# The gate and up products of a transformer layer by Strassen's seven block products in place of eight

## The chip, the cores and the metric

The kernel runs on one core of a Trainium2 chip. Its time is the device time of one launch in microseconds (us), the median of several runs. The engines are named as the profile names them: PE is TensorE's matmuls, PEld its weight loads, DVE is VectorE, ACT is ScalarE, POOL is GpSimd, and SP issues the DMAs.

## What is computed

The reference is a block of two trunk layers over 512 latent tokens and 256 context tokens of width 1024. Each layer has a mixing part (four head groups and an output projection) and a feed-forward part; the change lies in the feed-forward of the last layer, which handles the latent tokens alone:

```python
def swiglu(h, wg, wu, wd):
    return (jax.nn.silu(h @ wg) * (h @ wu)) @ wd

x = x + g2 * swiglu(modulate(rms_norm(x, g_ffn[l]), sh2, sc2), w_gate[l], w_up[l], w_down[l])
```

Here h is 512 x 1024, w_gate and w_up are 1024 x 2816 and w_down is 2816 x 1024, all in float32.

## The kernel before, in words

Activations lie feature-major: 128 features on the partitions, tokens along the free dimension. A float32 product is made of three matmuls (`mm3`, lines 63 to 67): each operand is split into a high part in the rounded format that TensorE takes (a copy on ScalarE) and a low part (the difference, on VectorE), and high x high, high x low and low x high are added up in PSUM. Weights are loaded into `raw` (three buffers of 128x512) and split into `w` tiles (six buffers, each with the high and the low part of 128x512); `wsplit`, lines 75 to 85, does both. Line 82 is the high part on ACT, line 83 the low part on DVE (in parts of the mixing on POOL). `split_to` (lines 91 to 93) does the same for data already in SBUF.

In the output projection of the mixing part (lines 917 to 924) eight column tiles `mt` are made one after the other. For each of them `residual` (line 911) adds the product to the stream, `Squares` (lines 284 and 285) adds up the squares for the norm, and `scaled` (lines 255 to 258) puts out the token tile `st` of 128 features, scaled, in high and low parts, with two columns that carry the shift. The norm's factor r is multiplied in behind the products, since it depends on the token alone.

The feed-forward (lines 941 to 977) goes in three blocks of hidden column tiles, 8, 7 and 7 of the 22 (`BLOCKS`, line 24). For each column tile `ft` it splits the gate and the up weights (four `w` tiles), and for the last layer each of the two products runs over eight feature tiles and two token halves of 256 and 258 columns, three matmuls each: 96 matmuls for a column tile. Lines 949 to 958 take the products out of PSUM, multiply by r, apply SiLU, add the shifts, multiply gate by up, and split the result into a hidden tile `h`. After a block follow the down products (lines 966 to 971), eight column tiles of 512 columns over the block's hidden tiles.

The order of the instructions on each engine is written by a scheduler ahead of time from the program's order, the buffers and its own estimates; on the chip each engine then runs its list in order and waits by semaphores. PSUM's eight banks are handed out in turn (`psum_any`).

Of the kernel before, what the change touches and what calls it, by code (L numbers as in the profile page):

```python
# [17 lines left out]
KT = 8  # L18
# [21 lines left out]
def hybrid_block(ctx: ExitStack, tc, t, out):  # L40
# [221 lines left out]
    def scaled_proj(w, h, cuts, pss, k):
        for (c0, c1, *_), ps in zip(cuts[0], pss):
            mm3(ps[:, :c1 - c0], wf(w, k, 0), wf(w, k, 1), h[:, 0, c0:c1], h[:, 1, c0:c1], k == 0, k == KT - 1)

    def shift_of(cuts, pss):
        sh = small.tile([128, 2], F32, tag="sh", name="sh")
# [119 lines left out]
    for l in range(DEPTH):  # L387
# [529 lines left out]
        for mt in range(KT):  # L917
            w = wsplit(t["wout"][l, mt])
            outs = proj_out(w, KT, mh, ORDER, [[["pj", "pj", "tq", "md", "sc", "sc", "pt", "po"], ["pj", "pj", "tq", "md", "sc", "sc", "pt", "po"]][l][(mt * len(segs) + i) % 8] for i in range(len(segs))])
            x = xs[mt]  # L920
            residual(x, outs, per_feature(m, 2, mt))
            sq.add(x)
            sh = per_feature(m, 3, mt)
            h.append(scaled(x, a[:, 1, mt], sh[:, 0:1].to_broadcast([128, 2]) if last else sh, segs))

        turn[0] = 0
        r = norm_spread(norm_scale(sq, segs), segs, ("po", "pt"))
# [12 lines left out]
        work = steps()  # L940
        for b0, b1 in BLOCKS:
            hid = []
            for ft in range(b0, b1):
                gu = [wsplit(t["wg"][l, ft]), wsplit(t["wu"][l, ft])]
                gps, ups = [[psum_any() for _ in range(2)] for _ in range(2)]
                for w, pss in zip(gu, (gps, ups)):
                    for k in range(KT):
                        scaled_proj(w, h[k], cuts, pss, k)
                shg, shu = shift_of(cuts, gps), shift_of(cuts, ups)
                hd = tile("h", [128, 2, NT], F32R)  # L950
                for (_, _, s0, s1, v, o), g_, u_ in zip(cuts[0], gps, ups):
                    n = s1 - s0
                    sg, up = tile("post", [128, 512])[:, :n], tile("post", [128, 512])[:, :n]
                    V.tensor_mul(sg, g_[:, o:o + n], r[:, s0:s1])
                    S.activation(sg, sg, AF.Silu, bias=shg[:, v:v + 1])
                    V.tensor_mul(up, u_[:, o:o + n], r[:, s0:s1])
                    V.scalar_tensor_tensor(up, up, shu[:, v:v + 1], sg, op0=OP.add, op1=OP.mult)
                    split_to(hd[:, 0, s0:s1], hd[:, 1, s0:s1], up)
                for _ in range(3):
                    next(work, None)  # L960
                hid.append(hd)
            final = b1 == FFT
            if final:
                sq = Squares(segs)
                hu = []
            for mt in range(KT):
                n = b1 - b0
                w = wsplit(t["wd"][l, mt][:, b0:b1].rearrange("p k c -> p (k c)"))
                outs = proj_out(w, n, hid, range(n))
                x = xs[mt]  # L970
                residual(x, outs, per_feature(m, 5, mt))
                if final and last:
                    nc.sync.dma_start(out[:, mt], x[:, :SEQ])
                elif final:
                    sq.add(x)
                    nc.sync.dma_start(xdram[:, mt], x[:, :SEQ])
                    hu.append(scaled(x, mods[1]["a"][:, 0, mt], mods[1]["m"][:, mt // 4, 0, mt % 4], segs))
# [45 lines left out]
def _layouts(i):  # L1023
# [42 lines left out]
    o["win_dv"] = featmajor(i["w_in"][:, :, 1792:2048], KT).reshape(L, 2, 128, 1024)  # L1066
    wo = np.concatenate([i["w_out"][:, swap], i["w_out"][:, 256:]], 1)
    o["wout"] = featmajor(wo, KT).reshape(L, KT, 128, 1024)
    o["wg"] = featmajor(i["w_gate"], KT).reshape(L, FFT, 128, 1024)
    o["wu"] = featmajor(i["w_up"], KT).reshape(L, FFT, 128, 1024)  # L1070
    o["wd"] = featmajor(i["w_down"], FFT)
    for n in ("a_q_gain", "a_k_gain", "d_q_gain", "d_k_gain", "a_sink", "b_v_gain"):
        o[n] = ac(i[n])
# [27 lines left out]
```

## Time and profile before

| | |
|---|---|
| median of 3 runs | 1574.88 us (1571.65 to 1575.27) |
| profiled execution | 1574.71 us, its span 1572.9 us |
| TensorE's mean granted clock | 0.987 of full speed |
| busy share of PE, DVE, ACT, POOL | 97%, 60%, 40%, 7% |
| matmuls | 10,210 |
| DMA | 163.42 MB, mean 104 GB/s |

An engine's busy share is a mean over the whole span; what bounds a stage is read from the stage. The profile's time of a matmul is longer than the distance to the next, since they are pipelined: the distance between starts is what a matmul costs. The same holds for operations of VectorE and ScalarE in a dense stretch.

### The profile page before, as it was taken

How to read it: one execution, taken by the hardware profiler on the slowest of the kernel's cores; microseconds unless marked ns; L12 is line 12 of the kernel's file. 1: busy time of each engine (PE TensorE's matmuls, PEld its weight loads, DVE VectorE, ACT ScalarE, POOL GpSimd, SP SyncE). 2: the span in 40 equal slices, each digit the busy share in tenths (PEclk: the TensorE clock that was granted, in tenths of full speed). 3: DMA queues.
4: the chain of work that ended last, by engine and by line, in shares of the span. 5: the costliest groups of instructions: out<-in, count | busy, mean ns of one | idle time of the engine just before them, and what ended most of it. 6: DMA issues, size and time to landing. Idle time of an engine off the chain costs nothing.

```text
span 1572.9 us, 26447 instructions
## 1 busy us (share of the span) xinstructions
PE 1531.0 (97%) x10210; PEld 1348.2 (86%) x10210; DVE 950.5 (60%) x2325; ACT 628.3 (40%) x1305; POOL 116.2 (7%) x107
## 2 busy tenths in 40 slices
PE   7889999999999999999999998799999999999999
PEld 4678888788888888888888887798879998998997
DVE  4796867586485624833384467878856543454453
ACT  5545665543322112221222344457654332332331
POOL 2430200000000000000000005622000000000000
PEclk9899999999999999999999999999999999999999
DMA  8342133442243323622272231212223233223223
GB/s 308 121 128 85 50 126 107 134 138 81 83 145 111 117 61 114 223 57 69 90 245 64 79 118 41 71 42 73 69 61 102 94 88 101 95 83 106 94 82 101
DMA packets 79326, 163.42 MB, mean 104 GB/s; under 512 B 12000, under 2 KB 17760, under 8 KB 79200
## 3 DMA queue, kind: packets, MB, share of 16 engines
q1 hardware_dynamic: 79200, 161.73, 32.4%
q8 instruction: 80, 1.31, 0.3%
q14 instruction: 46, 0.38, 0.1%
HBM read 157.50 MB, written 4.19 MB: 103 GB/s over the span
## 4 chain that ended last, share of the span: by engine, by line
PE 88%; DVE 7%; DMA 3%; ACT 1%; issue 1%; SPq 0%; ACTq 0%; DVEq 0%
PE pj L65 9%; PE pj L67 9%; PE pj L66 9%; PE sc L66 6%; PE sc L65 6%; PE sc L67 6%; PE tq L65 3%; PE tq L66 3%; PE tq L67 3%; PE po L66 3%; PE po L65 3%; PE po L67 3%; PE po L351 3%; PE pt L66 2%; PE pt L67 2%; PE pt L65 2%
## 5 line engine op out<-in xcount | busy, mean ns | idle before, releaser
L82 ACT ACTIVATE w<-raw 128x512 fp32r<-128x512 f32 x368 | 227.4, 622 | 632.6 <-PE sc L67 157.3
L83 DVE TENSOR_TENSOR w<-raw,w 128x512 fp32r<-128x512 f32 x336 | 227.9, 681 | 244.8 <-ACT w L82 244.4
L65 PE MATMUL pj<-w,h 128*128 128x256 f32 x480 | 142.5, 297 | 14.7 <-DVE post L498 8.4
L66 PE MATMUL pj<-w,h 128*128 128x256 f32 x480 | 141.1, 294 | 1.5 <-DVE w L83 1.5
L67 PE MATMUL pj<-w,h 128*128 128x256 f32 x480 | 141.3, 295 | 0.0
L65 PE MATMUL pj<-st,w 128*128 128x258 f32 (+2 forms) x384 | 120.5, 314 | 0.9 <-ACT st L255 0.7
L66 PE MATMUL pj<-st,w 128*128 128x258 f32 (+2 forms) x384 | 120.2, 313 | 1.1 <-DVE st L256 1.1
L65 PE MATMUL sc<-st,w 128*128 128x258 f32 (+2 forms) x384 | 119.9, 312 | 0.0
L66 PE MATMUL sc<-st,w 128*128 128x258 f32 (+2 forms) x384 | 119.9, 312 | 0.0
L67 PE MATMUL pj<-st,w 128*128 128x258 f32 (+2 forms) x384 | 119.5, 312 | 0.0
L67 PE MATMUL sc<-st,w 128*128 128x258 f32 (+2 forms) x384 | 118.9, 310 | 0.0
L65 PEld LDWEIGHTS pj<-w,h 128*128 128x128 f32 x480 | 95.9, 200 | 18.7 <-DVE post L498 9.2
L66 PEld LDWEIGHTS pj<-w,h 128*128 128x128 f32 x480 | 95.9, 200 | 3.3 <-DVE w L83 1.7
L67 PEld LDWEIGHTS pj<-w,h 128*128 128x128 f32 x480 | 95.4, 199 | 3.1 <-issue 3.0
L83 POOL TENSOR_TENSOR w<-raw,w 128x512 fp32r<-128x512 f32 x32 | 42.3, 1338 | 722.7 <-ACT w L82 715.4
L65 PEld LDWEIGHTS pj<-st,w 128*128 128x128 f32 x384 | 73.0, 190 | 8.0 <-ACT st L255 1.9
L66 PEld LDWEIGHTS pj<-st,w 128*128 128x128 f32 x384 | 72.9, 190 | 5.9 <-DVE st L256 1.3
L67 PEld LDWEIGHTS pj<-st,w 128*128 128x128 f32 x384 | 72.7, 190 | 5.6 <-issue 1.7
L65 PEld LDWEIGHTS sc<-st,w 128*128 128x128 f32 x384 | 73.1, 190 | 4.7
L66 PEld LDWEIGHTS sc<-st,w 128*128 128x128 f32 x384 | 72.9, 190 | 4.1
L67 PEld LDWEIGHTS sc<-st,w 128*128 128x128 f32 x384 | 72.4, 189 | 4.1
L65 PE MATMUL po<-st,w 128*128 128x512 f32 (+1 forms) x192 | 66.6, 347 | 0.0
(310 smaller groups left out, 4153.4 us busy)
## 6 DMA issues: line engine op xcount, KB each, us to landing
mraw<-in_wmod SPq DMA_DIRECT2D x80, 512.0 KB, 3.6
raw<-in_wg SPq DMA_DIRECT2D x88, 256.0 KB, 2.6
raw<-in_wu SPq DMA_DIRECT2D x88, 256.0 KB, 2.6
raw<-in_wd SPq DMA_DIRECT2D x64, 256.0 KB, 2.7
h<-in_wslab SPq DMA_DIRECT2D x16, 512.0 KB, 7.9
raw<-in_wout SPq DMA_DIRECT2D x32, 256.0 KB, 2.7
x<-in_xt SPq DMA_DIRECT2D x16, 384.0 KB, 5.5
raw<-in_wd SPq DMA_DIRECT2D x32, 192.0 KB, 2.4
```

What stands on the lines that cost most here:

```text
L65: T.matmul(ps, ah, bh, start=start, stop=False)
L66: T.matmul(ps, ah, bl, start=False, stop=False)
L67: T.matmul(ps, al, bh, start=False, stop=stop)
L82: S.activation(w[:, 0, :n], raw, AF.Copy)
L83: eng.tensor_sub(w[:, 1, :n], raw, w[:, 0, :n].bitcast(F32))
L351: T.matmul(o[64 * hh:64 * hh + 64, :128], vs[hh][lo:hi], pts[i, hh], start=i == 0, stop=i == n - 1)
```

## The change

For the last layer each pair of column tiles is handled at once. The weights of a pair form a 2x2 block matrix (two halves of the features by two column tiles), the tokens another one (two halves of the features by two halves of the tokens). The products of the blocks are made by Strassen's scheme in Winograd's form, seven products of sums and differences of blocks in place of eight products of blocks. To this end:

- The host's layout of the gate and up weights puts the feature tiles of one half next to each other, so that a 128x512 piece is one block. Layer 0 reads the same layout with another index (`at`).
- `token_blocks` and `token_forms` take the place of `scaled`: the four token blocks go into an `mraw` tile, GpSimd makes four differences of them (128x258) in a second one, and the seven operands are split into high and low parts.
- `weight_forms` loads the four weight blocks of a pair (two into an `mraw` tile in one DMA of 512 KB, two into `raw` tiles), makes four sums and differences of 128x512 on GpSimd in `pts` tiles (three buffers), and splits seven operands.
- `strassen` runs seven products of four feature tiles, three matmuls of 258 columns each, and puts four results together with seven additions out of PSUM on VectorE and one copy on ScalarE.
- The blocks of column tiles become 8, 8 and 6, for both layers.

Shortened:

```diff
-BLOCKS = ((0, 8), (8, 15), (15, 22))
+BLOCKS = ((0, 8), (8, 16), (16, 22))
...
+    def token_blocks(par, x, gain, sh, b):
+        S.activation(by128(b[:, 2 * par:2 * par + 2, 0:HN]), halves(x), AF.Copy, scale=gain[:, 0:1])
+        for h in (2 * par, 2 * par + 1):
+            V.tensor_copy(b[:, h, HN:HN + 2], sh[:, 0:1].to_broadcast([128, 2]))
+
+    def token_forms(b, single):
+        u = tile("mraw", [128, 4, HN + 2])
+        G.tensor_sub(u[:, 1], b[:, 1], b[:, 0])
+        G.tensor_sub(u[:, 2], b[:, 3], u[:, 1])
+        G.tensor_sub(u[:, 0], b[:, 2], u[:, 2])
+        G.tensor_sub(u[:, 3], b[:, 3], b[:, 1])
+        f1 = tile(single, [128, 1, 2, HN + 2], F32R)
+        f2 = tile("st", [128, 3, 2, HN + 2], F32R)
+        f3 = tile("st", [128, 3, 2, HN + 2], F32R)
+        for f, i, src in ((f2, 0, b[:, 2:4]), (f1, 0, b[:, 0:1]), (f3, 0, u[:, 1:4]), (f2, 2, u[:, 0:1])):
+            n = src.shape[1]
+            split_to(f[:, i:i + n, 0], f[:, i:i + n, 1], src)
...
+    def weight_forms(src):
+        both = load_raw(src[0], "mraw")
+        a11, a12 = both[:, 0:512], both[:, 512:1024]
+        a21, a22 = [load_raw(src[1][:, c:c + 512], "raw", 512) for c in (0, 512)]
...
+        yield parts(a12)
+        yield parts(a11)
+        s1 = comb(G.tensor_add, a21, a22)
+        yield parts(s1)
+        s2 = comb(G.tensor_sub, s1, a11)
+        yield parts(s2)
+        yield parts(comb(G.tensor_sub, a12, s2))
+        yield parts(a22)
+        yield parts(comb(G.tensor_sub, a11, a21))
+
+    def strassen(src, forms):
+        wfs = weight_forms(src)
+        n = HN + 2
+        def product(p):
+            ps = psum_any()[:, :n]
+            w = next(wfs)
+            for kk, f in enumerate(forms):
+                mm3(ps, w[:, 0, 128 * kk:128 * kk + 128], w[:, 1, 128 * kk:128 * kk + 128], *f[p],
+                    kk == 0, kk == len(forms) - 1)
+            return ps
+        c1, c2 = tile("post", [128, 2, n]), tile("post", [128, 2, n])
+        u = tile("br", [128, n])
+        p2, p1 = product(2), product(1)
+        S.activation(u, p1, AF.Copy)
+        V.tensor_add(c1[:, 0], p2, u)
+        p5, p6 = product(5), product(6)
+        V.tensor_add(u, p6, u)
+        V.tensor_add(c1[:, 1], p5, u)
+        p3 = product(3)
+        V.tensor_add(c1[:, 1], p3, c1[:, 1])
+        p4, p7 = product(4), product(7)
+        V.tensor_add(c2[:, 0], p7, u)
+        V.tensor_add(c2[:, 1], p5, c2[:, 0])
+        V.tensor_add(c2[:, 0], p4, c2[:, 0])
+        return c1, c2
...
-            h.append(scaled(x, a[:, 1, mt], sh[:, 0:1].to_broadcast([128, 2]) if last else sh, segs))
+            if not last:
+                h.append(scaled(x, a[:, 1, mt], sh, segs))
+                continue
+            if mt % 2 == 0:
+                blocks = tile("mraw", [128, 4, HN + 2])
+            token_blocks(mt % 2, x, a[:, 1, mt], sh, blocks)
+            if mt % 2:
+                h.append(token_forms(blocks, "T" if mt < 6 else "bias"))
...
+            for ft in range(b0, b1, 2) if last else ():
+                rv = halves(r)
+                gate = strassen([t["wg"][l, ft], t["wg"][l, ft + 1]], h)
+                for c in gate:
+                    cv = c[:, :, 0:HN]
+                    V.tensor_mul(by128(cv), by128(cv), rv)
+                    S.activation(cv, cv, AF.Silu, bias=c[:, 0, HN:HN + 1])
+                up = strassen([t["wu"][l, ft], t["wu"][l, ft + 1]], h)
+                for c, g_ in zip(up, gate):
+                    cv = c[:, :, 0:HN]
+                    V.tensor_mul(by128(cv), by128(cv), rv)
+                    V.scalar_tensor_tensor(cv, cv, c[:, 0, HN:HN + 1], g_[:, :, 0:HN], op0=OP.add, op1=OP.mult)
+                    hd = tile("h", [128, 2, NT], F32R)
+                    split_to(halves(hd[:, 0]), halves(hd[:, 1]), by128(cv))
+                    hid.append(hd)
```

In the lists that follow a row is one instruction with the line of the kernel that issues it, what it writes and reads by tile names, its shape, and the engines or DMA queues that it waits for; x2 stands for two alike.

VectorE in the middle of a gate/up stretch, one column tile of before (`w` are low halves of weights, line 954 and 956 the products with the norm, 957 gate by up):

```order
L83 TENSOR_TENSOR w<-raw,w 128x512 [waits DMAHW4_49,Activation_49]
L954 TENSOR_TENSOR post<-pj,row 128x256 [waits PE_49]
L268 COPY sh<-pj 128x2 [waits PE_49]
L83 TENSOR_TENSOR w<-raw,w 128x512 [waits DMAHW5_49,Activation_49]
L83 TENSOR_TENSOR w<-raw,w 128x512 [waits DMAHW6_49,Activation_49]
L956 TENSOR_TENSOR post<-sc,row 128x256 [waits PE_49]
L954 TENSOR_TENSOR post<-pj,row 128x256 [waits DVE_49]
L268 COPY sh<-sc 128x2 [waits PE_49]
L956 TENSOR_TENSOR post<-sc,row 128x256 [waits DVE_49]
L957 SCALAR_TENSOR_TENSOR post<-post,sh 128x256 [waits DVE_49]
L83 TENSOR_TENSOR w<-raw,w 128x512 [waits DMAHW7_49,Activation_49]
L957 SCALAR_TENSOR_TENSOR post<-post,sh 128x256 [waits DVE_49,Activation_49]
```

and the same place now, the second half of a pair (348 to 357 are the additions out of PSUM, 1054 the product with the norm, 1055 gate by up, `w<-pts` the low half of a sum that GpSimd made):

```order
L93 TENSOR_TENSOR w<-pts,w 128x512 [waits Activation_49]
L353 TENSOR_TENSOR post<-sc,post 128x258 [waits DVE_49,PE_49]
L1054 TENSOR_TENSOR post<-post,row 128x2x256 [waits DVE_49]
L93 TENSOR_TENSOR w<-pts,w 128x512 [waits Activation_49]
L1055 SCALAR_TENSOR_TENSOR post<-post 128x2x256 [waits DVE_49]
L93 TENSOR_TENSOR w<-pts,w 128x512 [waits Activation_49]
L355 TENSOR_TENSOR post<-pt,br 128x258 [waits PE_49]
L93 TENSOR_TENSOR w<-raw,w 128x512 [waits DMAHW6_49,Activation_49]
L356 TENSOR_TENSOR post<-pj,post 128x258 [waits DVE_49]
L93 TENSOR_TENSOR h<-post,h 128x2x2x128 [waits Activation_49]
L357 TENSOR_TENSOR post<-tq,post 128x258 [waits DVE_49]
L93 TENSOR_TENSOR w<-pts,w 128x512 [waits Activation_49]
```

Of twelve rows before, four are low halves of weights. Of twelve now five are, four of them of what GpSimd wrote, and four are additions of 128x258 with one input in PSUM.

GpSimd before, from its last work in the last layer's mixing part (low halves of projection weights, bias tiles) to the end of the program:

```order
L625 TENSOR_TENSOR bias<-dmask,br 128x256 [waits DMAHW1_49,DVE_49]
L625 TENSOR_TENSOR bias<-dmask,br 128x192 x2
L83 TENSOR_TENSOR w<-raw,w 128x512 [waits DMAHW0_49,Activation_49]
L83 TENSOR_TENSOR w<-raw,w 128x512 [waits DMAHW2_49,Activation_49]
L83 TENSOR_TENSOR w<-raw,w 128x512 [waits DMAHW3_49,Activation_49]
L1096 UNCONDITIONAL_BRANCH
L1096 ISA [waits barrier_Pool_Activation_PE_DVE_SP_gather]
```

and now, from the differences of the last token blocks into the first weight sums (`mraw<-mraw` token blocks, `pts` weight sums):

```order
L292 TENSOR_TENSOR mraw<-mraw 128x258 [waits DVE_49,Activation_49,Pool_49]
L293 TENSOR_TENSOR mraw<-mraw 128x258 [waits Activation_49,Pool_49]
L295 TENSOR_TENSOR mraw<-mraw 128x258
L294 TENSOR_TENSOR mraw<-mraw 128x258 [waits Pool_49]
L318 TENSOR_TENSOR pts<-pts,mraw 128x512 [waits DMAHW1_49,PE_49]
L318 TENSOR_TENSOR pts<-mraw,pts 128x512 [waits PE_49,Pool_49]
L318 TENSOR_TENSOR pts<-mraw,raw 128x512 [waits DVE_49]
L318 TENSOR_TENSOR pts<-raw 128x512 [waits DMAHW0_49,DMAHW3_49,DVE_49,Pool_49]
L318 TENSOR_TENSOR pts<-pts,mraw 128x512 [waits DMAHW2_49,DVE_49,Pool_49]
L318 TENSOR_TENSOR pts<-mraw,pts 128x512 [waits DVE_49,Pool_49]
```

Before, GpSimd's list ends with the projections of the mixing part; now eighty-eight weight sums follow, eight for each pair of column tiles.

SP's loads where the output projection passes into gate/up, before:

```order
L72 DMA raw<-in_wout 128x512 [waits DMAHW4_49,DMAHW0_49,DVE_49]
L72 DMA raw<-in_wout 128x512 [waits DMAHW5_49,DMAHW2_49,DVE_49]
L72 DMA raw<-in_wg 128x512 [waits DMAHW6_49,DMAHW3_49,DVE_49]
L72 DMA raw<-in_wg 128x512 [waits DMAHW7_49,DMAHW4_49,DVE_49]
L72 DMA raw<-in_wu 128x512 [waits DMAHW5_49,DVE_49]
L72 DMA raw<-in_wu 128x512 [waits DMAHW6_49,DMAHW1_49,DVE_49]
L72 DMA raw<-in_wg 128x512 [waits DMAHW7_49,DVE_49]
L72 DMA raw<-in_wg 128x512 [waits DMAHW0_49,DVE_49]
```

and now:

```order
L72 DMA raw<-in_wout 128x512 [waits DMAHW4_49,DMAHW0_49,DVE_49]
L72 DMA raw<-in_wout 128x512 [waits DMAHW5_49,DMAHW2_49,DVE_49]
L72 DMA raw<-in_wg 128x512 [waits DMAHW6_49,DMAHW3_49,DVE_49]
L72 DMA raw<-in_wg 128x512 [waits DMAHW7_49,DMAHW4_49,DVE_49]
L72 DMA raw<-in_wu 128x512 [waits DMAHW5_49,DVE_49]
L72 DMA mraw<-in_wg 128x1024 [waits DMAHW1_49,DVE_49,Pool_49]
L72 DMA mraw<-in_wu 128x1024 [waits DVE_49]
L72 DMA raw<-in_wu 128x512 [waits DMAHW6_49,Pool_49]
L72 DMA mraw<-in_wg 128x1024 [waits DMAHW1_49,DVE_49]
```

The first two gate loads stand where they stood. The 512 KB load of the first gate blocks (`mraw<-in_wg`) waits for VectorE and GpSimd, whose token blocks hold its buffer, and the loads of the later pairs stand behind it.

## Rows read from the trace of the kernel before

**Rows 1.** Part 1 of the page: busy us (share) and instructions of each engine.

```profile
PE 1531.0 (97%) x10210; PEld 1348.2 (86%) x10210; DVE 950.5 (60%) x2325; ACT 628.3 (40%) x1305; POOL 116.2 (7%) x107
```

**Rows 2.** Stages: us, busy us of PE, PEld, DVE, ACT, POOL; clock; DMA.

```profile
1194.46:1288.19 93.73, 93.73 (x785) 93.73 (x784) 48.38 (x118) 35.16 (x65) 0.00 (x0) 1.00 0.29 91
1331.77:1412.23 80.46, 80.46 (x674) 80.46 (x673) 39.26 (x92) 27.75 (x53) 0.00 (x0) 1.00 0.29 90
1450.36:1530.82 80.46, 80.46 (x674) 80.45 (x672) 39.27 (x92) 27.75 (x53) 0.00 (x0) 1.00 0.29 90
```

**Rows 3.** Timeline of PE in gate/up: start us, duration us, engine, line, operation.

```profile
1224.98 0.28 PE L65 MATMUL sc<-st,w 128*128 128x256 f32 x1
1230.73 0.28 PE L65 MATMUL tq<-st,w 128*128 128x256 f32 x1
```

**Rows 4.** Timeline of DVE in the output projection, a dense stretch.

```profile
1176.72 0.68 DVE L285 TENSOR_TENSOR row<-row 128x512 f32<-128x512 f32 x1
1177.32 0.74 DVE L256 SCALAR_TENSOR_TENSOR st<-x,a,st 128x512 fp32r<-128x512 f32 x1
1177.98 0.15 DVE L93 TENSOR_TENSOR st<-mod,st 128x2 fp32r<-128x2 f32 x1
```

**Rows 5.** Timeline of DVE, two products out of PSUM in a row.

```profile
1207.44 0.42 DVE L954 TENSOR_TENSOR post<-pj,row 128x256 f32<-128x256 f32 x1 [1.84 <-ACT row L303]
1207.78 0.41 DVE L956 TENSOR_TENSOR post<-sc,row 128x256 f32<-128x256 f32 x1
```

**Rows 6.** Timeline of POOL, three operations merged.

```profile
948.72 3.76 POOL L83 TENSOR_TENSOR w<-raw,w 128x512 fp32r<-128x512 f32 x3 [640.92 <-ACT w L82]
```

**Rows 7.** Timelines of DVE and POOL in the mixing part, both queued.

```profile
955.01 1.77 DVE L315 SCALAR_TENSOR_TENSOR x<-x,a,row 128x512 f32<-128x512 f32 x1
954.50 1.74 POOL L313 TENSOR_TENSOR x<-x,row 128x512 f32<-128x512 f32 x1
956.71 1.78 DVE L315 SCALAR_TENSOR_TENSOR x<-x,a,row 128x512 f32<-128x512 f32 x1
956.19 1.74 POOL L313 TENSOR_TENSOR x<-x,row 128x512 f32<-128x512 f32 x1
```

**Rows 8.** The same, with one input of DVE's operation in PSUM.

```profile
1000.43 1.28 POOL L83 TENSOR_TENSOR w<-raw,w 128x512 fp32r<-128x512 f32 x1
1000.60 0.42 DVE L498 TENSOR_TENSOR post<-pj,ry 128x256 f32<-128x256 f32 x1
```

**Rows 9.** Timelines where the output projection passes into gate/up.

```profile
1194.46 0.28 PE L65 MATMUL pj<-st,w 128*128 128x256 f32 x1
1194.66 0.75 DVE L911 SCALAR_TENSOR_TENSOR x<-po,mod,x 128x512 f32<-128x512 f32 x1 [1.36 <-PE po L67]
1195.50 0.63 ACT L284 ACTIVATE row<-x 128x512 f32<-128x512 f32 x1 [0.21 <-DVE x L911]
1196.04 0.71 ACT L255 ACTIVATE st<-x,a 128x512 fp32r<-128x512 f32 x1
```

**Rows 10.** Timeline of POOL, a 128x256 operation.

```profile
1015.42 0.74 POOL L625 TENSOR_TENSOR bias<-dmask,br 128x256 f32<-128x256 f32 x1 [8.06 <-PE sc L67]
```

**Rows 11.** DMA issues: issuer, count, KB each, median us from issue to landing.

```profile
mraw<-in_wmod SPq DMA_DIRECT2D x80, 512.0 KB, 3.6
raw<-in_wg SPq DMA_DIRECT2D x88, 256.0 KB, 2.6
```

**Rows 12.** Timeline of PE behind a gap, and the stage with its granted clock.

```profile
975.72 0.55 PE L65 MATMUL pj<-w,h 128*128 128x256 f32 x1 [6.22 <-DVE st L801]
980.13 0.41 PE L65 MATMUL pj<-w,h 128*128 128x256 f32 x1
980.34 0.41 PE L66 MATMUL pj<-w,h 128*128 128x256 f32 x1
980.98 0.28 PE L65 MATMUL pj<-w,h 128*128 128x256 f32 x1
976.00:980.00 4.00, 4.00 (x20) 4.00 (x20) 3.47 (x9) 1.64 (x4) 3.00 (x2) 0.50 0.00 0
```

More of the change, by code (lines that the diff above doesn't have):

```diff
@@ L260, in scaled, with scaled_proj, halves @@
         return hk
-    def scaled_proj(w, h, cuts, pss, k):
+    def scaled_proj(w, h, cuts, pss, k, at=None):
+        at = k if at is None else at
         for (c0, c1, *_), ps in zip(cuts[0], pss):
-            mm3(ps[:, :c1 - c0], wf(w, k, 0), wf(w, k, 1), h[:, 0, c0:c1], h[:, 1, c0:c1], k == 0, k == KT - 1)
+            mm3(ps[:, :c1 - c0], wf(w, at, 0), wf(w, at, 1), h[:, 0, c0:c1], h[:, 1, c0:c1], k == 0, k == KT - 1)
+    HN = SEQ // 2
+    def halves(x):
+        return x[:, :SEQ].rearrange("p (c h t) -> p h c t", h=2, t=128)
@@ new lines, in by128 @@
+    def by128(x):
+        return x.rearrange("p h (c t) -> p h c t", t=128)
+    def token_blocks(par, x, gain, sh, b):
[14 more added lines that the diff above has]
+            split_to(f[:, i:i + n, 0], f[:, i:i + n, 1], src)
+        at = {1: (f1, 0), 2: (f2, 0), 3: (f2, 1), 4: (f2, 2), 5: (f3, 0), 6: (f3, 1), 7: (f3, 2)}
+        return {p: (f[:, i, 0], f[:, i, 1]) for p, (f, i) in at.items()}
@@ new lines, in weight_forms, with parts, comb @@
+    def weight_forms(src):
+        both = load_raw(src[0], "mraw")
+        a11, a12 = both[:, 0:512], both[:, 512:1024]
+        a21, a22 = [load_raw(src[1][:, c:c + 512], "raw", 512) for c in (0, 512)]
+        def parts(x):
+            w = tile("w", [128, 2, 512], F32R)
+            split_to(w[:, 0], w[:, 1], x)
+            return w
+        def comb(f, x, y):
+            z = tile("pts", [128, 512])
+            f(z, x, y)
+            return z
+        yield parts(a12)
[7 more added lines that the diff above has]
+        yield parts(comb(G.tensor_sub, a11, a21))
@@ L942, in hybrid_block @@
             hid = []
-            for ft in range(b0, b1):
+            for ft in range(b0, b1, 2) if last else ():
[13 more added lines that the diff above has]
+                    hid.append(hd)
+            for ft in () if last else range(b0, b1):
                 gu = [wsplit(t["wg"][l, ft]), wsplit(t["wu"][l, ft])]
@@ L947, in hybrid_block @@
                     for k in range(KT):
-                        scaled_proj(w, h[k], cuts, pss, k)
+                        scaled_proj(w, h[k], cuts, pss, k, 4 * (k % 2) + k // 2)
                 shg, shu = shift_of(cuts, gps), shift_of(cuts, ups)
@@ L1068, in _layouts @@
     o["wout"] = featmajor(wo, KT).reshape(L, KT, 128, 1024)
-    o["wg"] = featmajor(i["w_gate"], KT).reshape(L, FFT, 128, 1024)
-    o["wu"] = featmajor(i["w_up"], KT).reshape(L, FFT, 128, 1024)
+    o["wg"], o["wu"] = [ac(featmajor(i[n], KT).reshape(L, FFT, 128, 4, 2, 128).transpose(0, 1, 2, 4, 3, 5))
+                        .reshape(L, FFT, 128, 1024) for n in ("w_gate", "w_up")]
     o["wd"] = featmajor(i["w_down"], FFT)
```

## The prediction

> **What bounds the kernel now.** I read the page's first part, then a table of the last layer's feed-forward by stage, then the timeline inside it. TensorE is busy 97% of the span and GpSimd 7% [rows 1]. The three gate/up stretches of the last layer (8, 7 and 7 column tiles) take 93.73, 80.46 and 80.46 us, 254.65 together, with TensorE busy in every microsecond at full clock, VectorE about half busy and GpSimd not at all [rows 2]. So here the time is the number of matmuls times their interval. The first matmul of a product pair and the first of the next stand 48 matmuls and 5.75 us apart, 0.1198 us each, whether 256 or 258 columns move [rows 3]. A column tile (gate and up, 96 matmuls) is 11.5 us, two of them 23.0.
>
> **What is removed.** Two column tiles needed 192 matmuls; Strassen's two sets of seven products need 2 x 7 x 4 x 3 = 168 of 258 columns. Over eleven pairs that is 264 matmuls fewer, 264 x 0.1198 = 31.6 us, if TensorE stays the bound: 20.1 us a pair. The down products are regrouped (8, 8, 6 in place of 8, 7, 7), their number stays, and so does layer 0's.
>
> **What is added on VectorE, per pair of column tiles.** The costs are distances between starts in a dense stretch: a 128x512 operation with both inputs in SBUF 0.60 us, a scalar_tensor_tensor of that size 0.66 [rows 4]; a 128x256 one with one input in PSUM 0.34 [rows 5]. The order shows for a pair: 14 low halves of weight forms (before: 8) 8.5, 14 additions out of PSUM 4.8, 4 products with the norm 2.4, 2 scalar_tensor_tensors 1.3, 2 low halves of the hidden tiles 1.2. Sum 18.2 us. With 0.5 for results that the very next instruction needs (6 or 7 places, under 0.1 each) 18.7: below the 20.1 of TensorE. ScalarE has about 19 operations of at most 0.7 us [rows 9], 12 us, and waits for nobody long. So far the change would win.
>
> **What is added on GpSimd, and what it does to VectorE.** Each pair brings 8 sums and differences of 128x512 on an engine that had nothing here. Three such operations in a row take 3.76 us [rows 6], so 1.25 each and 10 us per pair: beside TensorE's 20.1 that alone would be hidden. But an operation of GpSimd and one of VectorE with two SBUF inputs don't run together. Where both engines have them queued they alternate: GpSimd's starts stand 1.69 us apart and VectorE's 1.70, and a VectorE operation that needs 0.66 is recorded as 1.77 [rows 7]. So one GpSimd operation costs VectorE 1.70 - 0.66 = 1.04 us. One with an input in PSUM is not held: 0.42 us in the middle of a GpSimd operation [rows 8]. Of VectorE's 36 operations per pair 22 are held, 14 (the additions) are not.
> The Trainium skill says of this (SBUF — State Buffer, "Who interferes with whom") that the loser blocks for the whole instruction of the other. By that rule each GpSimd operation would cost its full 1.25 us where the cycle of [rows 7] gives 1.04; over the 76 operations counted below the sum would come out 16 us later, near 1595 us.
> What one costs here: 1.04 if the next VectorE operation is a held one, 1.04 - 0.34 = 0.70 if it is an addition, 0.35 with two. I went through the order of one pair with these prices, placing each GpSimd operation by the buffer or the load that it waits for: 0.95, 0.70, 0.70, 0.70, 1.00, 0.70, 0.35, 0.70, together 5.8. I take 0.75 each, 6.0 per pair; bounds 1.04 (no addition beside any) and about 0 (all fall into waits of VectorE). VectorE then needs 18.7 + 6.0 = 24.7 us per pair: more than TensorE's 20.1 and more than the 23.0 of before. It becomes the bound, TensorE waits for low halves, and ScalarE, GpSimd and the loads run ahead by their buffers (six weight tiles, three sums), so that VectorE waits for none of them.
>
> **The stretches.** VectorE's queue has seven weight forms ahead of the first addition, and at a stretch's end TensorE goes on into the down products while VectorE still has 15 operations to do. What stands between is, for four pairs, 49 low halves 29.4, 48 additions 16.3, 13 products 7.8, 6 scalar_tensor_tensors 4.0, 6 hidden halves 3.6, together 61.1, 2.0 for dependent results and 28 x 0.75 = 21.0 for GpSimd: 84.1 us. For three pairs: 35 x 0.60 + 34 x 0.34 + 9 x 0.60 + 4 x 0.66 + 4 x 0.60 = 43.0, 1.5, and 20 x 0.75 = 15.0: 59.5. The last product adds 1.5. Before it, the second and third stretch have their first forms ready under the down products, and the two first products take 2 x 1.44 plus 0.5 for ScalarE's copy: 3.4. So 89.0 for the second, 64.4 for the third.
>
> **The start of the first stretch.** Before, TensorE goes without a gap from the output projection into gate/up at 1194.46 [rows 9]: weights were there and seven of eight token tiles too. Now the first weight load of the gate goes into a tile pair that the token blocks of the projection's last two tiles still hold, and its DMA stands behind GpSimd's last difference and VectorE's split. The chain from 1194.46: residual, square and scaled copy end 2.3 later [rows 9]; three differences at 0.75 [rows 10], 2.5 with their waits; the 512 KB load 3.6 [rows 11]; high and low half 0.63 + 0.69: 9.7 us. Ahead of it three pairs of token blocks pass through two buffers, and GpSimd's queue has between them a sum of the first gate weights, whose load waits for the projection's own weight tiles; I estimate from the order that this puts VectorE's last residual 2 us behind its matmuls. I take 11.7 (9.7 to 14). What covered the seam (42 matmuls on ready tiles) is gone.
> After a gap of 6.22 us TensorE came back at half its clock (granted 0.50, 1.2 GHz, in that stretch) and a 256-column matmul took 0.21 [rows 12]. With the same here the first two products take 24 x 0.213 = 5.1 us and 1.0 for the first low half and the copy: 6.1. First stretch: 11.7 + 6.1 + 84.1 + 1.5 = 103.4.
>
> **Sum.** 103.4 + 89.0 + 64.4 = 256.8 against 254.65: +2.2. Three changes from gate/up to down, where the last hidden tile comes later than before but by the order more than 30 down matmuls on earlier tiles stand in front of it: +0.5 each, +1.5. The profiled execution took 1574.71 us (span 1572.9), 0.2 under the median of the runs shown. Forecast 1574.7 + 3.7, rounded up for waits of VectorE that I priced at nothing: 1579.
>
> **Rivals.**
> First: TensorE stays the bound, because the sums on GpSimd fall into idle moments of VectorE. For it: VectorE is only half busy in these stretches now [rows 2], and its own work is under 20.1. Against: 18.7 of 20.1 leaves 1.4 us of idle time per pair for 10 us of GpSimd. Price: first stretch 11.7 + 2.3 (24 half-clock matmuls) + 80.5, then 80.5 and 60.4: 235.4, or 19.2 less than now: 1555.
> Second, on the slower side: no addition stands beside a GpSimd operation, every one costs 1.04. It decides on VectorE's queue, where a GpSimd operation is let in only behind a held one; from 0.84 per operation on, the kernel is slower by more than 0.7%. For it: the alternation in [rows 7] is strict, and two to three sums come in a row. Against: ten groups of additions stand among the 22 held operations. Price: 76 x 0.29 = +22, 1601; with a start at 14 us 1603.
> Third: the clock falls in the stretches themselves, since TensorE would idle one to two us twice per pair. The gap that brought it down was 6.22 us [rows 12]; I give it 3%. Price: 168 x 0.213 = 35.8 us per pair in place of 24.7, +120.
> That the change leaves the matmuls where they were is excluded by the order: 84 per seven products.
>
> **How the numbers follow.** Forecast 50% (own range 1570 to 1589), first rival 22%, second 25%, third 3%. What the measurement can tell from no change is 0.3%, 4.7 us. The forecast's half splits into 0.04 faster, 0.24 same, 0.22 slower; the first rival gives 0.20 faster and 0.02 same; the others are slower. Together 0.24, 0.26, 0.50. Range: from 1557, short of the first rival's price, to 1603, the second's with the late start; some 2 in 10 lie outside.
>
> **What would show it.** In the stretches VectorE near 100% with low halves recorded at 1.1 to 1.8 us beside GpSimd, about 24.7 us from one pair to the next, and TensorE's idle time ending on VectorE. A gap of TensorE of 10 to 14 us near 1195 that ends on a load, and a clock of 0.50 behind it. The second and third stretch near 89 and 64. I am wrong if low halves keep 0.69 beside GpSimd's sums, if a pair takes 20 us, or if the gap is closed by other work.

## The result: slower by 1.3%, inside the range and 14 us above the forecast

The changed kernel takes 1592.94 us (1591.17 to 1596.03, 4 runs), the kernel before 1573.29 us (1571.65 to 1575.27, 4 runs). The ratio is 1.0126, interval 1.0104 to 1.0149, or +19.7 us. Forecast was 1579, +4, with slower as the likeliest side; the result lies above the forecast's own range (1570 to 1589) and below the second rival's 1601. The profiled execution took 1591.17 us, its span is 1589.1.

The first row of the page, against [rows 1], shows 264 matmuls fewer and 19 us less of TensorE, while VectorE and GpSimd have 140 us more each:

```profile
PE 1511.8 (95%) x9946; PEld 1322.0 (83%) x9946; DVE 1091.0 (69%) x2429; ACT 668.1 (42%) x1357; POOL 258.4 (16%) x211
```

The three gate/up stretches, each from the end of the matmuls ahead of it to the first down product (columns as in [rows 2]):

```profile
1189.60:1299.23 109.63, 90.52 (x689) 88.20 (x689) 103.75 (x161) 51.60 (x92) 50.16 (x37) 0.92 0.29 90
1344.03:1438.14 94.11, 85.33 (x673) 84.12 (x672) 91.45 (x136) 43.32 (x78) 38.03 (x27) 0.96 0.29 89
1482.94:1551.68 68.74, 62.85 (x506) 62.05 (x504) 65.96 (x101) 32.30 (x58) 26.49 (x19) 0.98 0.24 72
```

Where [rows 2] had TensorE busy in every microsecond, TensorE now idles 9 us in the second stretch and VectorE under 3. The three sum to 272.48 us against 254.65: +17.8. Between and behind them (first down product to the next stretch or the end) lie 44.80 + 44.80 + 37.42 = 127.0 us, before 43.58 + 38.13 + 42.08 = 123.8: +3.2. Together +21.0. The profile of after reached the end of the output projection 4.9 us earlier than that of before (1189.60 against 1194.46), so the spans differ by 16.2 only. I don't count that to the change: in the profiles of its variants below this point lies anywhere from 1188.0 to 1194.5.

What TensorE waits for there (matmul, releaser: us in total, times, longest):

```profile
PE pj L65 <- DVE post L356: 8.0, 3, 3.3
PE tq L386 <- DVE row L379: 5.4, 1, 5.4
PE po L65 <- DVE post L356: 4.5, 3, 2.2
PE md L65 <- DVE post L356: 4.1, 3, 1.4
PE po L395 <- DVE ry L109: 3.3, 1, 3.3
PE md L67 <- DVE w L93: 3.2, 3, 1.1
```

L356 is an addition that has to free a PSUM bank, L93 a low half of a weight form, L379 and L109 the norm at the start. All are VectorE. L379 and L109 are why one sign fails as it was put: the idle time before the first product was to end on a load, and in the profile it ends on VectorE.

### The profile page after: what moved, and what is told of

Read it like the earlier page. It is cut to its first block, busy times and chain, and to the rows that moved or that the text cites. A ratio compares the mean times of both kernels' runs of the same rounds, so it can differ in the third digit from the quotient of the medians.

```text
span 1589.1 us, 26222 instructions
## 1 busy us (share of the span) xinstructions
PE 1511.8 (95%) x9946; PEld 1322.0 (83%) x9946; DVE 1091.0 (69%) x2429; ACT 668.1 (42%) x1357; POOL 258.4 (16%) x211
## 4 chain that ended last, share of the span: by engine, by line
PE 72%; DVE 16%; issue 4%; DMA 3%; ACT 2%; POOL 2%; SPq 0%; POOLq 0%; ACTq 0%; DVEq 0%
PE pj L65 7%; PE pj L66 7%; PE pj L67 7%; DVE w L93 4%; PE sc L66 4%; PE sc L65 4%; PE sc L67 4%; PE po L445 3%; PE tq L65 3%; PE tq L66 3%; PE tq L67 3%; PE po L65 3%; PE po L66 3%; PE po L67 3%; PE md L65 2%
## 5 line engine op out<-in xcount | busy, mean ns | idle before, releaser
L82 ACT ACTIVATE w<-raw 128x512 fp32r<-128x512 f32 (+1 forms) x280 | 171.1, 618 | 431.3 <-PE pj L67 102.0
L83 DVE TENSOR_TENSOR w<-raw,w 128x512 fp32r<-128x512 f32 x248 | 165.8, 675 | 69.9 <-ACT w L82 69.0
L65 PE MATMUL pj<-w,h 128*128 128x256 f32 x480 | 140.7, 294 | 15.0 <-DVE post L592 8.6
L66 PE MATMUL pj<-w,h 128*128 128x256 f32 x480 | 139.4, 291 | 2.0 <-DVE w L83 2.0
L67 PE MATMUL pj<-w,h 128*128 128x256 f32 x480 | 139.5, 291 | 0.4 <-DVE h L411 0.4
L65 PE MATMUL pj<-st,w 128*128 128x512 f32 (+2 forms) x344 | 110.6, 322 | 9.6 <-DVE post L356 8.0
L66 PE MATMUL pj<-st,w 128*128 128x512 f32 (+2 forms) x344 | 109.8, 319 | 1.8 <-DVE st L256 1.8
L65 PEld LDWEIGHTS pj<-w,h 128*128 128x128 f32 x480 | 94.1, 196 | 19.2 <-DVE post L592 9.4
L66 PE MATMUL sc<-st,w 128*128 128x512 f32 (+2 forms) x344 | 109.0, 317 | 0.0
L67 PE MATMUL pj<-st,w 128*128 128x512 f32 (+2 forms) x344 | 108.8, 317 | 0.2 <-DVE w L93 0.2
L65 PE MATMUL sc<-st,w 128*128 128x512 f32 (+2 forms) x344 | 108.9, 317 | 0.0
L67 PE MATMUL sc<-st,w 128*128 128x512 f32 (+2 forms) x344 | 108.1, 315 | 0.0
L93 DVE TENSOR_TENSOR w<-pts,w 128x512 fp32r<-128x512 f32 x88 | 83.4, 952 | 11.2 <-ACT w L92 11.2
L65 PEld LDWEIGHTS pj<-st,w 128*128 128x128 f32 x344 | 66.2, 193 | 18.2 <-ACT w L92 5.1
L92 ACT ACTIVATE h<-post 128x512 fp32r<-128x512 f32 x66 | 34.7, 555 | 98.4 <-DVE post L1055 63.5
L92 ACT ACTIVATE w<-pts 128x512 fp32r<-128x512 f32 x88 | 53.5, 625 | 45.4 <-POOL pts L318 16.0
L66 PEld LDWEIGHTS pj<-st,w 128*128 128x128 f32 x344 | 66.2, 192 | 6.7 <-DVE st L256 2.1
L67 PEld LDWEIGHTS pj<-st,w 128*128 128x128 f32 x344 | 66.0, 192 | 4.6 <-DVE w L93 0.5
L65 PEld LDWEIGHTS sc<-st,w 128*128 128x128 f32 x344 | 66.0, 192 | 4.5
```

The costliest lines, as they stand in the source:

```text
L82: S.activation(w[:, 0, :n], raw, AF.Copy)
L83: eng.tensor_sub(w[:, 1, :n], raw, w[:, 0, :n].bitcast(F32))
L92: S.activation(hi, src, AF.Copy)
L93: V.tensor_sub(lo, src, hi.bitcast(F32))
```

## How a sum on GpSimd holds VectorE

A dense piece of VectorE's timeline in the second stretch (start, duration, line, operation), then GpSimd's over the same time:

```profile
1368.50 1.45 DVE L93 TENSOR_TENSOR h<-post,h 128x512 fp32r<-128x512 f32 x1
1369.88 0.41 DVE L357 TENSOR_TENSOR post<-tq,post 128x258 f32<-128x258 f32 x1
1370.21 1.44 DVE L93 TENSOR_TENSOR w<-pts,w 128x512 fp32r<-128x512 f32 x1
1371.58 0.68 DVE L1054 TENSOR_TENSOR post<-post,row 128x512 f32<-128x512 f32 x1
1372.18 0.41 DVE L348 TENSOR_TENSOR post<-po,br 128x258 f32<-128x258 f32 x1
1372.52 1.45 DVE L93 TENSOR_TENSOR w<-mraw,w 128x512 fp32r<-128x512 f32 x1
1373.89 0.74 DVE L1055 SCALAR_TENSOR_TENSOR post<-post 128x512 f32<-128x512 f32 x1
...
1376.09 0.41 DVE L351 TENSOR_TENSOR post<-pj,br 128x258 f32<-128x258 f32 x1
1376.42 1.66 DVE L93 TENSOR_TENSOR h<-post,h 128x512 fp32r<-128x512 f32 x1
1378.01 0.68 DVE L93 TENSOR_TENSOR w<-pts,w 128x512 fp32r<-128x512 f32 x1
```

```profile
1369.48 1.63 POOL L318 TENSOR_TENSOR pts<-pts,mraw 128x512 f32<-128x512 f32 x1
1371.80 1.61 POOL L318 TENSOR_TENSOR pts<-mraw,pts 128x512 f32<-128x512 f32 x1 [0.69 <-DVE w L93]
1376.24 1.29 POOL L318 TENSOR_TENSOR pts<-mraw,raw 128x512 f32<-128x512 f32 x1 [2.83 <-DVE w L93]
```

The additions out of PSUM (L357, L348, L351) keep their 0.41 beside a GpSimd operation, as in [rows 8]. The two-input operation behind each of them runs until about half a microsecond after GpSimd's end (1371.11, 1373.41, 1377.53). The one at 1370.21 is followed after 1.37 us in place of 0.60: 0.77 lost, with one addition in front. The sum at 1376.24 begins 0.15 after an addition's start, so less of it lies under that, and 0.99 is lost. A pair's period is read from the first addition of one pair (L348) to that of the next; the first three rows that follow are the first additions of the three stretches, the last two are further pairs of the second.

```profile
1208.94 0.41 DVE L348 TENSOR_TENSOR post<-pj,br 128x258 f32<-128x258 f32 x1
1347.54 0.43 DVE L348 TENSOR_TENSOR post<-pj,br 128x258 f32<-128x258 f32 x1 [0.45 <-ACT br L347]
1486.45 0.43 DVE L348 TENSOR_TENSOR post<-pj,br 128x258 f32<-128x258 f32 x1 [0.45 <-ACT br L347]
1396.48 0.41 DVE L348 TENSOR_TENSOR post<-tq,br 128x258 f32<-128x258 f32 x1
1421.91 0.41 DVE L348 TENSOR_TENSOR post<-sc,br 128x258 f32<-128x258 f32 x1
```

With the row at 1372.18 the periods of the second stretch are 24.64, 24.30 and 25.43 us, 24.8 on average, where 24.7 was forecast. What GpSimd costs VectorE can be added up from the timeline: for each operation that is recorded longer than undisturbed, the distance to the next start, less the 0.60 or 0.66 that it takes undisturbed. In the second stretch 26 operations are held for 22.2 us, in the third 18 for 14.9, in the first 29 (from its first product on) for 25.0: 62.1 us over 73 operations, 0.85 each, from 0.30 to 1.11 in the second stretch. Forecast was 0.75.

## The experiments

All are medians; kernels in one group ran on the same chip beside the kernel before (1573.5 us in the first, 1574.2 in the second, 1573.8 in the third). The changed kernel is taken at its 1592.9.

**First group: the regrouping, the sums, the seam.**

```diff
 # kernel before
-BLOCKS = ((0, 8), (8, 15), (15, 22))
+BLOCKS = ((0, 8), (8, 16), (16, 22))
```

> The kernel before with the column tiles in blocks of 8, 8 and 6 in place of 8, 7 and 7, nothing else. Theory (the regrouping is worth nothing, the loss comes from the seven products): the same as before within 2 us, 1571 to 1576. Rival (part of the loss, or of the 4.9 us by which the changed kernel reaches the end of the output projection earlier, is the regrouping's): more than 3 us away from before, on either side.

Measured 1574.0, ratio 1.0001 (0.9988 to 1.0015). The regrouping is worth nothing, as forecast.

```diff
 # changed kernel, weight_forms
         def comb(f, x, y):
-            z = tile("pts", [128, 512])
-            f(z, x, y)
-            return z
+            return x
```

> The changed kernel with the four weight sums left out: the plain weight block stands where a sum or difference of blocks stood (so four of seven products are made of other weights), GpSimd has nothing to do in gate/up, and everything else is as in the changed kernel. Theory (VectorE is the bound because each of GpSimd's sums costs it 0.75 to 0.9 us): VectorE needs 18.7 us per pair, TensorE's 20.1 becomes the bound, the three stretches shrink from 272.5 to about 240 us, 1560 (1554 to 1567). Rival (the loss lies in the start of the stretch and in chains from TensorE over VectorE back to TensorE, and the sums cost nothing): within 5 us of the changed kernel, 1588 to 1598.

Measured 1557.7, ratio 0.9898 (0.9878 to 0.9918): 35 us less than the changed kernel. The stretches of this kernel:

```profile
1194.53:1288.10 93.57, 86.06 (x690) 85.81 (x689) 82.02 (x164) 55.04 (x94) 3.25 (x4) 0.95 0.36 109
1332.90:1413.59 80.69, 80.69 (x674) 80.69 (x673) 72.44 (x137) 46.06 (x78) 0.00 (x0) 1.00 0.36 109
1458.38:1518.88 60.50, 60.50 (x506) 60.49 (x504) 53.50 (x101) 33.65 (x58) 0.00 (x0) 1.00 0.30 91
```

TensorE is the bound again, 80.69 us for four pairs or 20.2 a pair, with nearly the same number of operations on VectorE (137, before the edit 136). So nothing else that the change adds to VectorE is too much; these are the stretches that the first rival forecast (94.5, 80.5, 60.4).

```diff
-        s1 = comb(G.tensor_add, a21, a22)
+        s1 = comb(V.tensor_add, a21, a22)     # and so for the three differences
```

> The changed kernel with its 88 weight sums on VectorE in place of GpSimd. They cost VectorE 88 x 0.60 = 53 us there. Theory (on GpSimd they cost it 0.78 to 0.9 us each, 69 to 79 us): 16 to 26 us faster than the changed kernel, 1567 to 1577. With 1.04 us each, the price of strict alternation: 39 us faster, 1554. Rival (on GpSimd they are hidden): 30 to 53 us slower, 1623 to 1646.

Measured 1570.2, ratio 0.9979 (0.9966 to 0.9993). With the same sums, but at 0.60 us each in its own queue, VectorE is 22.7 us sooner done: 0.60 + 22.7 / 88 = 0.86 us is what one cost on GpSimd, as a mean over all 88; 12 of them run under the down products, where VectorE has time to spare, and over the other 76 it is 0.60 + 22.7 / 76 = 0.90. The 0.85 of the timeline lies beside it. The edit isn't a pure price: in this run TensorE's list has some 18 down matmuls of a block ahead of the last products of each longer stretch (from 1289.74 and from 1422.01), where the changed kernel has none.

```diff
 # token_forms
-        u = tile("mraw", [128, 4, HN + 2])
-        G.tensor_sub(u[:, 1], b[:, 1], b[:, 0])
+        u, v = tile("post", [128, 2, HN + 2]), tile("post", [128, 2, HN + 2])
+        V.tensor_sub(u[:, 0], b[:, 1], b[:, 0])    # and so for the three others
```

> The changed kernel with the token differences written to other buffers (post tiles), so that the first gate load of 512 KB need not wait for the last token blocks, and made on VectorE in place of GpSimd. Theory (the gap of 12.2 us before the first product ends on that load, as forecast): the gap shrinks to about 6 us, bounded by the last token tile's residual, copy, differences and halves; 1585 to 1589. Rival (the gap is set by the last token forms and by VectorE's queue, the load is only the last to come): within 2 us of the changed kernel, 1591 to 1595.

Measured 1585.2, ratio 1.0071 (1.0050 to 1.0091): 7.8 us gained at the seam, of a gap that shrinks from 12.2 to under 4 us. TensorE's two seams, the changed kernel first (idle time and its releaser in brackets):

```profile
1189.20 0.40 PE L67 MATMUL po<-h,w 128*128 128x512 f32 x1
1194.96 1.86 PE L386 MATMUL tq<-ones,row 128*128 128x1 f32 x8 [5.36 <-DVE row L379]
1200.12 2.08 PE L395 MATMUL po<-ident,ry 128*128 128x128 f32 x8 [3.30 <-DVE ry L109]
1201.85 0.56 PE L65 MATMUL pj<-st,w 128*128 128x258 f32 x1
```

```profile
1192.73 0.40 PE L67 MATMUL po<-h,w 128*128 128x512 f32 x1
1195.74 1.05 PE L386 MATMUL tq<-ones,row 128*128 128x1 f32 x8 [2.61 <-DVE row L379]
1196.65 0.37 PE L65 MATMUL pj<-st,w 128*128 128x258 f32 x1
```

**Second group: both edits, and another order.** Since VectorE is the bound in gate/up and half idle under the down products, the two stages can be mixed. In the interleaved kernels the last layer goes in six blocks, `downs` is a generator that makes one down column tile at a time, and two are taken behind each set of seven products:

```diff
+LAST = ((0, 4), (4, 8), (8, 12), (12, 16), (16, 20), (20, 22))
...
+        pend = iter(())
+        for b0, b1 in LAST if last else BLOCKS:
...
                 gate = strassen([t["wg"][l, ft], t["wg"][l, ft + 1]], h)
...
+                for _ in range(2):
+                    next(pend, None)
                 up = strassen([t["wu"][l, ft], t["wu"][l, ft + 1]], h)
...
+                for _ in range(2):
+                    next(pend, None)
...
+            for _ in pend:
+                pass
+            pend = downs(b0, b1, hid)
```

> The two edits together: token differences in other buffers and on VectorE, and the 88 weight sums on VectorE. Theory (the two losses lie in different places and add up): 1592.9 - 22.7 - 7.8 = 1562 (1560 to 1565). Rival (VectorE is full at the seam too, so that the earlier load only lets it start on sums that delay the last token forms): no gain over the sums alone, 1568 to 1571.

Measured 1569.3, ratio 0.9966 (0.9950 to 0.9981). The sum of the two gains didn't come: 1 us below the sums alone, which the two intervals can't tell apart; the rival had the size, but its reason isn't what the windows below show. TensorE does start 8 us sooner after the projection, and loses it again 20 us later. Windows of this kernel (columns as in [rows 2]):

```profile
1208.00:1212.00 4.00, 2.05 (x15) 1.63 (x14) 3.40 (x10) 1.76 (x4) 0.00 (x0) 1.00 0.77 257
1212.00:1216.00 4.00, 3.25 (x13) 2.95 (x14) 3.11 (x6) 1.94 (x3) 0.00 (x0) 0.52 0.16 48
1216.00:1220.00 4.00, 3.48 (x17) 3.19 (x16) 2.21 (x6) 1.65 (x4) 0.00 (x0) 0.50 0.45 160
```

TensorE idles for 3.2 of these 12 us, its clock is granted at about 0.50 in the last eight, and there VectorE is busy for 3.1 and 2.2 us of four. The wait ends on the norm's chain (its spread over the tokens starts at 1212.07, 24.1 us behind the end of the projection; in the changed kernel 10.5); that this chain is the cause I haven't tested.

> The changed kernel, sums on GpSimd as there, with six blocks of 4, 4, 4, 4, 4 and 2 column tiles, and the down products of a block written between the gate/up products of the next (two of the eight behind each set of seven products). Theory (VectorE is the bound in gate/up and half idle under the down products, so that mixing the two stages evens it out): VectorE's work of the last feed-forward is 11 x 24.8 + 64 + 24 residuals of 0.66 = 353 us, TensorE's 341, so 1189.6 + 12.3 + 353 + 5 = 1560 and 1562 with what lies around the span (1552 to 1568). Rival (the seven products wait for chains of results, not for VectorE's load, or the weight buffers keep the two stages apart): 24 residuals more, 1593 to 1609.

Measured 1563.6, ratio 0.9935 (0.9912 to 0.9957): 29 us below the changed kernel, faster than before, with the sums still on GpSimd.

> The interleaved order with the token differences in other buffers and on VectorE. Theory: what the seam gave by itself, 7.8 us, below the interleaved kernel: 1554 (1545 to 1561). Rival (interleaving leaves TensorE so little to spare that the seam's gain is given back later): within 2 us of the interleaved kernel.

Measured 1557.8, ratio 0.9894 (0.9872 to 0.9917): 5.8 us less, within the range, though its interval just overlaps that of the interleaved kernel.

> The interleaved order, the seam edit, and the weight sums on VectorE. Theory: VectorE 11 x 23.5 + 64 + 16 = 338 us, TensorE 341 us: TensorE is the bound again over the whole feed-forward, 1189.6 + 6 + 341 + 5 + 2 = 1544 (1541 to 1553), faster than both kernels. Rival (neither engine can be kept full, since each set of seven products ends in additions that the other engine waits for): 1555 to 1563, no better than the seam and the sums alone.

Measured 1554.2, ratio 0.9870 (0.9851 to 0.9888): the fastest, 20 us below before and 39 below the changed kernel, though 10 above the theory's point, outside its range and just below the rival's. Its interval overlaps that of the kernel above. Its feed-forward, the start and the part behind it:

```profile
1191.13:1268.21 77.08, 71.75 (x546) 68.89 (x545) 74.83 (x152) 42.05 (x73) 0.00 (x0) 0.98 0.34 110
1268.21:1519.28 251.07, 251.07 (x1731) 233.73 (x1729) 232.14 (x419) 115.08 (x193) 0.00 (x0) 1.00 0.32 98
```

For 251 us TensorE is busy throughout at full clock, and VectorE has 19 us to spare. In the first 77, where there are few down products yet to mix in, TensorE idles for 5.3 us; the rest of the 10 us I can't place.

**Third group: price, seam and control.**

```diff
             f(z, x, y)
+            f(z, x, y)
             return z
```

> The changed kernel with each of its 88 weight sums written twice in a row on GpSimd, the same values into the same tile. GpSimd's work per pair doubles to 16 operations and some 26 us. Theory (VectorE bounds the stretches, and a sum costs it about 0.94 us there, the period of 26.2 us less its own 18.7, over 8): 66 to 88 more of them cost 62 to 83 us, 1655 to 1676. With 0.75 us each, as forecast: 1592.9 + 50 to 66, 1643 to 1659. Rival (the sums are not what slows VectorE): within 10 us of the changed kernel, as long as GpSimd's 26 us per pair don't become the bound themselves.

Measured 1687.0, ratio 1.0721 (1.0700 to 1.0741): +94.1 us for 88 sums, 1.07 each, above my range. Not all of this is time that GpSimd holds VectorE. The second stretch (1385.21 to 1509.39) grows by 30.1 us. VectorE is held for 44.1 us there over 51 operations, 0.86 each, in place of 22.2 over 26, which gives 21.9; its idle time grows from 2.6 to 10.8, which gives 8.2, and ends mostly on TensorE's products. So 1.07 is what a sum more costs here with these waits. While GpSimd has the next sum queued, its starts are 1.52 to 1.70 apart and VectorE gets one two-input operation through between two of them, as in [rows 7]; the first row below, VectorE's, is two such operations in 3.07 us.

```profile
1402.47 3.15 DVE L93 TENSOR_TENSOR w<-mraw,w 128x512 fp32r<-128x512 f32 x2
1401.93 1.44 POOL L318 TENSOR_TENSOR pts<-raw 128x512 f32<-128x512 f32 x1 [3.33 <-DMA raw<-in_wg]
1403.45 1.61 POOL L319 TENSOR_TENSOR pts<-raw 128x512 f32<-128x512 f32 x1
1405.15 1.63 POOL L318 TENSOR_TENSOR pts<-pts,mraw 128x512 f32<-128x512 f32 x1
1406.85 1.62 POOL L319 TENSOR_TENSOR pts<-pts,mraw 128x512 f32<-128x512 f32 x1
```

The two halves of the seam edit, each alone (the buffers changed with `G.tensor_sub` kept; `V.tensor_sub` with the `mraw` tile kept):

> The changed kernel with the token differences in other buffers (so that the first gate load is early) but still on GpSimd. Theory (the gap ends on the load): most of the seam's 7.8 us, 1585 to 1588. Rival (what counts is that VectorE is held by the token differences on GpSimd): within 2 us of the changed kernel, 1591 to 1595.

> The changed kernel with the token differences on VectorE but in the buffers of the changed kernel, so that the first gate load still waits for the last token blocks. Theory of the load: within 3 us of the changed kernel, 1589 to 1595. Rival (VectorE's queue at the seam, held by 16 differences on GpSimd at up to 0.9 us each): 5 to 8 us faster, 1585 to 1588.

Measured 1586.3 (ratio 1.0079, 1.0061 to 1.0097) and 1587.3 (1.0083, 1.0063 to 1.0103): 6.6 and 5.6 us gained, 7.8 together. Either half alone gives most of the gain, and the three intervals overlap. With the load early, the first product starts 3 us after the projection in place of 12.2, but the first stretch, from the end of the projection, shrinks only from 109.6 to 105.4: once TensorE has started, it waits for VectorE. The 12.2 us gap was never worth 12.2.

The control of the interleaved order, the six blocks without the mixing (`LAST` as above, nothing else):

> The control for the interleaved order: the changed kernel with the same six blocks of 4, 4, 4, 4, 4 and 2 column tiles in the last feed-forward, the down products of a block behind its own gate/up products as before. Theory (the gain of the interleaved kernel, 29 us, is that of mixing the stages, and small blocks alone only add 24 residuals and more changes of stage): 1593 to 1615. Rival (smaller blocks are what helps, since VectorE catches up under the down products six times in place of three): 1560 to 1580.

Measured 1578.3, ratio 1.0028 (1.0017 to 1.0039). My theory for this one fell: small blocks alone give 14.6 of the 29.3 us, the mixing the other 14.7. The four blocks of two pairs, from one first product after the down products to the next, take (1538.58 - 1273.07) / 4 = 66.4 us each; without the 96 down matmuls at 0.228 (the 192 of the 44.80 us above take 43.7) that is 44.5, or 22.2 a pair. In the second block of the changed kernel it is (94.11 + 44.80 - 43.7) / 4 = 23.8. My reading, which no run tests: a block of four column tiles has more of its VectorE work in its neighbours' down products, by what six weight tiles can hold ahead and by what is left at its end.

## Why the forecast was right in kind and short in size

- **What bounds the stretches.** VectorE, as forecast; it idles under 3 of 94 us in the second stretch. Shown by no_sums (TensorE the bound, 35 us less) and by sums_on_vectore (the same work without GpSimd's share, 22.7 less).
- **The ends of the stretches.** This is the term that was mis-sized: "The last product adds 1.5." The forecast let VectorE's part end where 15 of its operations are left and gave TensorE one product behind it. TensorE's last wait does end there, on L356 with those 15 left, but TensorE has three products and a rest to run from then on, some 40 matmuls on record. They take 4.80, 6.31 and 6.46 us. The terms of the three stretches, forecast first and then measured (us):

| | first stretch | second | third |
|---|---|---|---|
| start | 11.7, 12.25 | | |
| to the first addition | 6.1, 7.09 | 3.4, 3.51 | 3.4, 3.51 |
| VectorE's part, to TensorE's last wait | 84.1, 85.49 | 84.1, 84.29 | 59.5, 58.77 |
| end | 1.5, 4.80 | 1.5, 6.31 | 1.5, 6.46 |
| sum | 103.4, 109.63 | 89.0, 94.11 | 64.4, 68.74 |

So the ends hold 13.1 of the 15.7 us by which the stretches are longer than forecast. This is read from the profile; no run changes the ends alone. TensorE at its last waits, then from there to the first down product (columns as in [rows 2]):

```profile
1294.43 0.39 PE L65 MATMUL tq<-st,w 128*128 128x258 f32 x1 [0.77 <-DVE post L356]
1431.83 0.39 PE L65 MATMUL tq<-st,w 128*128 128x258 f32 x1 [0.77 <-DVE post L356]
1545.22 0.58 PE L65 MATMUL po<-st,w 128*128 128x258 f32 x1 [1.13 <-DVE post L356]
```

```profile
1294.43:1299.23 4.80, 4.80 (x39) 4.80 (x40) 4.72 (x10) 2.32 (x5) 0.00 (x0) 1.00 0.48 125
1431.83:1438.14 6.31, 6.31 (x39) 6.31 (x40) 5.74 (x12) 3.19 (x7) 0.00 (x0) 0.73 0.53 147
1545.22:1551.68 6.46, 6.46 (x43) 6.46 (x43) 5.72 (x13) 3.27 (x7) 0.00 (x0) 0.77 0.42 122
```

- **Price of a sum.** "I take 0.75 each, 6.0 per pair" was somewhat low: 0.85 measured. It moved the time little. VectorE's own operations in its part come to 61.1 and 42.7 us in the second and third stretch, as forecast (61.1 and 43.0), and it is held there for 22.2 and 14.9 us where 28 and 20 sums at 0.75 made 21.0 and 15.0: the price was too low and the number of sums (26 and 18) too high. That the two cancel in the third is luck.
- **The second rival.** Its 1.04 each is 0.19 too high. That 1601 lies nearer to the result than 1579 comes from the ends of the stretches, which neither had.
- **The rule on the port.** The Trainium skill's rule (SBUF — State Buffer, "SBUF: two separate sides"), that the loser blocks for the whole instruction of the other, agrees with the timeline above. There VectorE's operations at 1370.21, 1372.52 and 1376.42 end 0.54 to 0.56 us behind GpSimd's, whenever they were started. The 1595 us that I worked out from it was the nearest of all, by luck: it puts 0.21 on each sum's 0.75, 0.96 in place of 0.85, and that stands in for the missing ends.
- **The start.** 11.7 us were forecast from [rows 9 to 11], 12.2 measured, and the chain is the one named: residual at 1192.77, square and scaled copy to 1194.80, GpSimd's three differences to 1197.50, the load to 1200.97. But TensorE's idle time in it ends on the norm (L379 and L109), whose last matmuls stand right ahead of the first product, and it is not all loss (above). From 1203.3 on the matmuls are 0.12 us apart, so the half clock forecast for the first two products was there for little more than a microsecond; the 7.09 us to the first addition are VectorE's, with six low halves, two of them held for 2.2 us.
- **Changes of stage.** +3.2 us in place of +1.5.
- **The clock.** The third rival's chance rested on one gap of 6.22 us [rows 12]. The clock did fall in the stretches, as after a gap of 3.29 us (below). In their middle that cost little, since TensorE wasn't the bound. At the ends it was: 39 matmuls take 6.31 us in the second stretch in place of 4.80 at full clock in the first, 1.5 more.

```profile
1231.69 0.58 PE L65 MATMUL pj<-st,w 128*128 128x258 f32 x1 [3.29 <-DVE post L356]
1231.70:1236.00 4.30, 4.30 (x20) 4.30 (x21) 4.30 (x6) 1.19 (x3) 3.53 (x3) 0.50 0.20 64
```

- **The regrouping.** Nothing, as forecast, and shown alone.

Put together: +2.2 forecast for the stretches, 13.1 for the ends of the stretches, 2.6 for the rest of them, 3.2 at the changes of stage, 21.1, beside the 21.0 of the stage table and the 19.7 of the medians.

## What to carry to other kernels

A helper engine whose operations hold another engine's isn't free at any load: price each of its operations by what the other engine loses. Here some 0.85 us lost on VectorE, between the 0.75 by the order and the 1.04 of strict alternation, bought what VectorE does itself in 0.60. Price the end of a stretch as well: ask how much the waiting engine still has to run, and at which clock, once the engine that holds it lets go. And when a change moves the bound from one engine to another in one stage, look for the stage beside it where the new bound is idle: mixing the two, in smaller blocks, turned 1.3% slower into 0.6% faster with the sums still on GpSimd; the smaller blocks alone gave half of that.

## What was not expected of the hardware

- Gaps of TensorE well below the 6.22 us of [rows 12] brought the clock down: two of 1.05 (at 1404.53) and 2.19 us (at 1407.47) with 0.75 us of matmuls between them left it at 0.59 on average over the next 4 us. Single gaps of 2.39 us (at 1382.60) and 1.37 us (at 1393.22) did not; both stretches behind them read 1.00:

```profile
1382.60:1386.60 4.00, 4.00 (x33) 4.00 (x34) 4.00 (x6) 2.37 (x5) 2.27 (x2) 1.00 0.23 70
1393.20:1397.20 4.00, 3.98 (x33) 3.98 (x34) 4.00 (x5) 1.83 (x4) 3.22 (x3) 1.00 0.22 70
1407.50:1411.50 4.00, 4.00 (x21) 4.00 (x22) 4.00 (x6) 0.73 (x2) 2.00 (x2) 0.59 0.23 66
```

- The lengths of the gaps alone don't tell: ahead of the ends shown above, gaps of 1.42 and 0.77 us left the clock at 1.00 in the first stretch, and gaps of 1.00 and 0.77 were followed by 0.73 on average over the next 6.31 us in the second.
- GpSimd's operations are stretched as well as VectorE's: a 128x512 sum is mostly recorded at 1.27 to 1.30 us where VectorE has an addition under way at its start and at 1.6 to 1.74 where it has a two-input operation.
